# Half-width products in seven for the gate tiles of the first mixer and the up tiles of the second FFN, and a plain down projection behind them

## The chip, the cores and the metric

The kernel runs on one core of one Trainium2 chip. The metric is the device time of one execution in microseconds (us). Engines are named as in the profile: PE (TensorE, the matmuls), PEld (its weight loads), DVE (VectorE), ACT (ScalarE), POOL (GpSimd) and SP (SyncE, which here only issues the loads of weights).

## What is computed

The input is a row of 512 tokens with 1024 features, all in fp32. Two blocks follow each other. The change touches these lines of the first one:

```python
h = h + 0.5 * swiglu(rms_norm(h, ffn1_norm), ffn1_w1, ffn1_w3, ffn1_w2)
u = rms_norm(h, mix_norm)
s5_in, q, k, v, r, a_low, g_s5, g_gla = split(u @ w_in)      # g_s5, g_gla: 1024 columns each
...
merged = sigmoid(g_s5) * (y_s5 @ proj_s5) + sigmoid(g_gla) * (y_gla @ proj_gla)
h = h + merged @ w_out
h = h + 0.5 * swiglu(rms_norm(h, ffn2_norm), ffn2_w1, ffn2_w3, ffn2_w2)

def swiglu(x, w1, w3, w2):            # D_FF = 2816
    return (silu(x @ w1) * (x @ w3)) @ w2
```

The second block is another mixer and a third FFN; the change leaves them alone.

## The kernel before

Features lie on the partitions and tokens on the free axis, so that an activation of 1024 features is eight tiles of 128x512 and the 2816 features of an FFN are 22 such tiles. Every fp32 product is made of three fp32r matmuls (`mm3`): each operand is split into a rounded high part and the rest, and high by high, high by low and low by high are added up in PSUM. All of these matmuls have the line of one helper, L408. For weights the split costs work on two engines: SP loads a "raw" tile of up to 1024 columns (three buffers), ACT casts it to "wh" (four buffers), and DVE subtracts the cast from the raw tile and leaves "wl" (four buffers). The product of one output tile with eight input tiles is 24 matmuls of 512 columns into one of four PSUM banks (tag "mm").

The normalisation's factor rB is not applied to the inputs of a product (hgh, hgl: the input times the norm's weights, split) but when its result is read out of PSUM. So a tile of the second FFN (`up_tile`) is: 24 matmuls for w1, 24 for w3, DVE multiplies each by rB ("ua", "ub"), ACT makes silu of the first ("us"), DVE multiplies the two. A gate tile of the first mixer (`gate`) is 24 matmuls, a multiplication by rB on DVE and a sigmoid on ACT.

There is a second form of product in the kernel, `seven`: a block of two output tiles by two input tiles, with the 512 tokens cut in two halves, is a 2x2 matrix product of blocks, and it is made of seven half-width products (256 columns) in place of eight. Before the products, DVE makes sums and differences of the four weight blocks ("ws", two buffers) and of the two input tiles (T1 to T4; `Pairs.put`); after them, sums of the seven results. P7 and P4 share a PSUM bank, as do P5 and P3, and P1 and P2, so that the first of each must be read before the second starts. Before the change this form stands only in the down projections of the three FFNs: `gated` makes the up tiles in parts of four (`PARTS`), and each part of four tiles is multiplied by w2 in four `down_pair` of one `seven` each, spread between the next part's up tiles; the last six of the 22 tiles (`REST`) go plain.

The order of the instructions on each engine isn't that of the code. A recorder takes down every operation with a cost, and `schedule` is a list planner: it gives each engine the first operation by class (URGENT, MAIN, BACK) and program order whose inputs and buffers are ready by the costs. The order is static: on the chip each engine runs its list in order and waits for semaphores. In the first mixer the gate tiles are MAIN work, between which the small fp32 matmuls of the GLA branch (BACK) are laid one by one.

The stages lie in the trace as follows: first FFN to 312 us, first mixer to 695.5 (its gate tiles' matmuls from 490 to 598, then the S5 output, the two projections and w_out), second FFN to 1054, second mixer to 1417, third FFN to the end.

Of the kernel before, what the change touches and what calls it, by code (L numbers as in the profile page):

```python
# [1668 lines left out]
```

## Time and profile before

| | us |
|---|---|
| median of three runs | 1789.58 (1789.54 to 1789.81) |
| the profiled execution, its own time | 1789.26 |
| its span, first to last instruction | 1787.5 |
| PE busy | 1772.5 (99%) |
| DVE busy | 1344.0 (75%) |
| ACT busy | 889.4 (50%) |
| granted TensorE clock, mean | 0.997 |

A matmul's duration in the trace (395 ns for 512 columns) overlaps the next one's; what a matmul costs in a row of them is the distance between two starts. On DVE and ACT, too, an instruction often starts a little before the one ahead of it has ended. "Idle before, releaser" says how long an engine sat idle before a group of instructions and what ended that.

### The profile page before, as it was taken

Reading aid. Unit: us, or ns where it says so; the run is one execution under the profiler, and the core shown is the slowest. Engines: PE = TensorE matmul, PEld = TensorE weight load, DVE = VectorE, ACT = ScalarE, POOL = GpSimd, SP = SyncE. Lnnn points to the kernel's source line nnn. Section 1 sums busy time; section 2 is a strip of 40 time slices with the busy share of each in tenths; the row PEclk is TensorE's granted clock in tenths of the full one; section 3 lists DMA queues with packets and bytes.
Section 4 is the critical chain, followed back from the end, with each engine's and each line's share of the span. In section 5 each row is a group of like instructions: output and inputs, shape, how many; then the busy total and the mean of one; then the engine's idle time right before and its main releaser. Section 6 shows DMA issues by size and latency. Waiting matters only on the chain. (4 is left out here: it accounts for less than half of the span.)

```text
span 1787.5 us, 23941 instructions
## 1 busy us (share of the span) xinstructions
PE 1772.5 (99%) x9010; PEld 1510.7 (85%) x9010; DVE 1344.0 (75%) x2516; ACT 889.4 (50%) x1179; POOL 96.2 (5%) x180
## 2 busy tenths in 40 slices
PE   9999999999999999999999999999999999999997
PEld 7888888878888888888888888888888888888886
DVE  8899999659674475667777589788856578887875
ACT  6454444432853334333333354999953454554443
POOL 0011111211100000000000001000000000000000
PEclk9999999999999999999999999999999999999998
DMA  7455555665322342233333335232234444454551
GB/s 246 119 153 160 150 151 171 195 216 171 107 69 80 98 141 95 86 98 100 97 97 103 95 112 165 83 98 91 85 105 147 118 118 130 124 136 131 140 142 47
DMA packets 75636, 222.09 MB, mean 124 GB/s; under 512 B 8736, under 2 KB 17728, under 8 KB 75520
## 3 DMA queue, kind: packets, MB, share of 16 engines
q1 hardware_dynamic: 62304, 175.68, 30.4%
q0 software_dynamic: 13072, 44.87, 10.4%
q8 instruction: 71, 1.16, 0.3%
q14 instruction: 45, 0.37, 0.1%
q10 hardware_dynamic: 144, 0.00, 0.0%
HBM read 182.77 MB, written 15.73 MB: 111 GB/s over the span
## 5 line engine op out<-in xcount | busy, mean ns | idle before, releaser
L408 PE MATMUL mm<-hgh,wh 128*128 128x512 f32 x1528 | 602.9, 395 | 0.5 <-DVE ua L355 0.5
L408 PE MATMUL mm<-hgl,wh 128*128 128x512 f32 x1528 | 602.3, 394 | 0.0
L408 PE MATMUL mm<-hgh,wl 128*128 128x512 f32 x1520 | 598.9, 394 | 0.0
L400 ACT ACTIVATE wh<-raw 128x1024 fp32r<-128x1024 f32 (+2 forms) x315 | 310.0, 993 | 568.2 <-PE mm L408 322.5
L408 PEld LDWEIGHTS mm<-hgh,wh 128*128 128x128 f32 x1528 | 286.7, 188 | 58.4 <-DVE ua L355 0.9
L408 PEld LDWEIGHTS mm<-hgh,wl 128*128 128x128 f32 x1520 | 285.6, 188 | 58.5 <-issue 0.2
L408 PEld LDWEIGHTS mm<-hgl,wh 128*128 128x128 f32 x1528 | 286.5, 188 | 57.0 <-issue 0.2
L355 DVE TENSOR_TENSOR wl<-raw,wh 128x1024 fp32r<-128x1024 f32 (+2 forms) x272 | 306.6, 1128 | 34.0 <-ACT wh L400 33.4
L355 DVE TENSOR_TENSOR h<-mm,h 128x256 f32<-128x256 f32 (+1 forms) x134 | 66.2, 497 | 52.5 <-PE mm L408 51.6
L400 ACT ACTIVATE wh<-ws 128x1024 fp32r<-128x1024 f32 x48 | 50.7, 1056 | 83.1 <-PE mm L408 79.8
L400 ACT ACT_TABLE_LOAD x63 | 80.8, 1283 | 2.9 <-PEq L1659 1.2
L355 DVE TENSOR_TENSOR ub<-mm,rB 128x512 f32<-128x512 f32 x44 | 30.4, 691 | 64.0 <-PE mm L408 63.9
L355 DVE TENSOR_TENSOR ua<-mm,rB 128x512 f32<-128x512 f32 x54 | 37.3, 690 | 52.5 <-PE mm L408 51.0
L367 DVE SCALAR_TENSOR_TENSOR y<-t,vec,y 128x511 f32<-128x511 f32 x88 | 65.7, 747 | 7.8 <-ACT y L400 6.9
L421 POOL DMA_DIRECT2D wl<-raw x42 | 36.6, 872 | 605.4 <-ACT wl L400 464.1
L355 DVE TENSOR_TENSOR t<-mm,rB 128x512 f32<-128x512 f32 x44 | 30.4, 690 | 49.7 <-PE mm L408 49.5
L355 DVE TENSOR_TENSOR h<-h,mm 128x256 f32<-128x256 f32 x144 | 59.6, 414 | 1.6 <-PE mm L408 1.5
L355 DVE TENSOR_TENSOR wl<-ws,wh 128x1024 fp32r<-128x1024 f32 x48 | 58.6, 1221 | 1.8 <-ACT wh L400 1.8
L355 DVE TENSOR_TENSOR gate<-mm,rB 128x512 f32<-128x512 f32 x32 | 22.0, 688 | 44.1 <-PE mm L408 43.6
L408 PE MATMUL mm<-x1h,wl 128*128 128x256 f32 x192 | 54.3, 283 | 0.0
L408 PE MATMUL mm<-x1l,wh 128*128 128x256 f32 x192 | 54.3, 283 | 0.0
L408 PE MATMUL mm<-x1h,wh 128*128 128x256 f32 x192 | 54.3, 283 | 0.0
(358 smaller groups left out, 3404.6 us busy)
## 6 DMA issues: line engine op xcount, KB each, us to landing
raw<-in_ffn_w_dram SPq DMA_DIRECT2D x84, 512.0 KB, 3.5
raw<-in_w_in_dram SPq DMA_DIRECT2D x62, 512.0 KB, 3.4
raw<-in_w_up_dram SPq DMA_DIRECT2D x44, 512.0 KB, 3.8
wl<-raw POOLq DMA_DIRECT2D x42, 512.0 KB, 4.5
raw<-in_ffn_w_s_dram SPq DMA_DIRECT2D x32, 512.0 KB, 4.4
raw<-in_w_out_dram SPq DMA_DIRECT2D x16, 512.0 KB, 3.3
raw<-in_w_down_s_dram SPq DMA_DIRECT2D x16, 512.0 KB, 4.8
s5w<-dram POOLq DMA_DIRECT2D x28, 256.0 KB, 4.5
```

The lines of the kernel that those rows point to most:

```text
L355: R.op("dve", dve1(o), lambda: nc.vector.tensor_tensor(out=o, in0=a, in1=b, op=op), [o], [a, b])
L367: R.op("dve", dve1(o) + 0.06 * len(_aps(s)), lambda: nc.vector.scalar_tensor_tensor(out=o, in0=a, scalar=s, in1=b, op0=op0, op1=op1), [o], ...
L400: R.op("act", c, lambda: nc.scalar.activation(o, i, f, **kw), [o], _aps(i, scale, bias), table=TABLES.get(f), cls=cls, after=after)
L408: R.op("pe", c, lambda: nc.tensor.matmul(ps, a, b, start=start, stop=stop, **kw), [ps], [a, b])
L421: R.op("pool", 1.04, lambda: nc.gpsimd.dma_start(o, i, accum_op=ALU.add), [o], [i, o], nbytes=4.0 * _size(o) * o.shape[0], lat=2.5)
```

## The change

Two stages get the seven-product form where they had plain products, and one loses it.

- `forms` makes the sums of the eight normalised input tiles once for a stage: for each of the four pairs of tiles, DVE adds high and low part back together (fa, fb), makes T1 to T4 in four half-width operations, and ACT and DVE split them.
- `pair8` makes two output tiles with all eight inputs by seven products of 12 half-width matmuls each. It loads two raw tiles of 512 KB, makes two tiles of weight sums, and splits four weight tiles (HW1, HA, HW2, HB). P7, P4 and P1 are copied out of PSUM by ACT, the others are read by DVE.
- First mixer: gate tiles 0 to 3 stay plain, 4 to 15 are six `pair8`.
- Second FFN: of the 22 up tiles six stay plain; the other 16 are eight pairs, each a `pair8` for w1 and one for w3. Its down projection is plain throughout, in five parts (`DOWN`); a part's four pairs of output tiles are taken up one at a time after the following up tiles or `pair8`, the last part at the end.

The first and third FFN and the second mixer keep their code; the weights are laid out for the new loads.

```diff
+    def forms(xs, after):
+        res = []
+        cut = lambda hl, o: (hl[0][:, o:o + HALF], hl[1][:, o:o + HALF])
+        for a_, b_ in zip(xs[0::2], xs[1::2]):
+            a, b, t1, t2 = slot("fa"), slot("fb"), slot("t1"), slot("t2")
...
+            add(b, b_[0], b_[1])
+            sub(t1[:, 0:HALF], a[:, 0:HALF], a[:, HALF:])
+            sub(t1[:, HALF:], b[:, HALF:], a[:, HALF:])
+            stt(t2[:, 0:HALF], t1[:, 0:HALF], -1.0, b[:, HALF:], ALU.mult, ALU.subtract)
+            stt(t2[:, HALF:], t2[:, 0:HALF], -1.0, b[:, 0:HALF], ALU.mult, ALU.subtract)
+            h1, h2 = split(t1, "x1"), split(t2, "x2")
...
+    def pair8(src, xs, rB):
+        c = 512
+        r1, r2 = new("raw", "raw"), new("raw", "raw")
+        dma("sp", r1, src[:, 0:2 * c])
+        dma("sp", r2, src[:, 2 * c:4 * c])
+        w1 = new("ws", "ws")
...
+        tt(v2(w1), v2(r2), r1[:, 0:c].unsqueeze(1).to_broadcast([128, 2, c]), ALU.add)
+        HW1 = split_of(w1, 2 * c)
+        HA = split_of(r2, 2 * c)
+        w2 = new("ws", "ws")
+        add(w2[:, 0:c], w1[:, 0:c], r2[:, c:2 * c])
+        add(w2[:, c:2 * c], w2[:, 0:c], r1[:, c:2 * c])
+        HW2 = split_of(w2, 2 * c)
+        HB = split_of(r1[:, c:2 * c], c)
...
+        def p6(ps):
+            add(V, ps, V)
+            tt(x3, x3, v3, ALU.add)
+            stt(x1, x1, -1.0, rB, ALU.mult, ALU.mult)
+        def p3(ps):
+            add(x0[:, hi], ps, V)
+            mul(x0[:, hi], x0[:, hi], rB[:, hi])
+        read = {"P7": lambda ps: act(x1[:, hi], ps, AF.Copy), "P5": lambda ps: add(x1[:, hi], ps, x1[:, hi]),
+                "P4": lambda ps: act(x1[:, lo], ps, AF.Copy), "P1": lambda ps: act(V, ps, AF.Copy),
+                "P6": p6, "P3": p3, "P2": lambda ps: mul(x0[:, lo], ps, rB[:, lo])}
+        for key, (h, l), o, x, bank, more in (
+                ("P7", HW1, c, "T3", "D", False), ("P5", HW1, 0, "T1", "C", False),
+                ("P4", HA, 0, "T4", "D", True), ("P1", HA, c, "B11", "A", False),
+                ("P6", HW2, 0, "T2", "B", False), ("P3", HW2, c, "B22", "C", True),
+                ("P2", HB, 0, "B21", "A", True)):
...
+    UP0 = 6
+    DOWN = ((0, 4), (4, 8), (8, 12), (12, 16), (16, NFF))
+    def swiglu_pairs(hg, rB, h, done):
...
+        xs = forms(hg, [rB])
+        for n in range(UP0):
+            a.append(split(up_tile("ffn2_w1", "ffn2_w3", n, hg, rB), "g"))
...
+        for i in range((NFF - UP0) // 2):
+            us = pair8(A["ffn2_w1_g"][i], xs, rB)
+            for u in us:
+                act(u, u, AF.Silu)
+            if jobs:
+                down(*jobs.pop(0))
+            vs = pair8(A["ffn2_w3_g"][i], xs, rB)
...
-    swiglu("ffn2_w1", "ffn2_w3", "ffn2_w2", hg0, rB, h, both)
+    swiglu_pairs(hg0, rB, h, both)
...
-    g5 = [gate(i) for i in range(8)]
-    gg = [gate(8 + i) for i in range(8)]
+    xs = e.forms(hg, [G["r"][3]])
+    for i in range(6):
+        for x in e.pair8(e.A["w_in_g"][i], xs, rB):
+            act(x, x, AF.Sigmoid)
+            gates.append(x)
```

How the lists of the engines look at the places of which the prediction speaks (in brackets the engines and DMA queues whose semaphores a row waits for). First DVE while the later gate tiles are made; x are a gate pair's two tiles, V the shared partial sum, ws the weight sums. Before:

```order
L355 TENSOR_TENSOR ygl_1064<-o_1057,ygh_1063 128x512 [waits DMASW5_49,Activation_49]
L355 TENSOR_TENSOR gate_1105<-mm_1106,rB_813 128x512 [waits PE_49]
L355 TENSOR_TENSOR wl_1129<-raw_1127,wh_1128 128x1024 [waits DMAHW5_49,Activation_49]
L355 TENSOR_TENSOR gate_1110<-mm_1111,rB_813 128x512 [waits PE_49]
L355 TENSOR_TENSOR wl_1134<-raw_1132,wh_1133 128x1024 [waits DMAHW6_49,Activation_49]
L355 TENSOR_TENSOR gate_1115<-mm_1116,rB_813 128x512 [waits PE_49]
L355 TENSOR_TENSOR wl_1139<-raw_1137,wh_1138 128x1024 [waits DMAHW7_49,Activation_49]
```

Now:

```order
L355 TENSOR_TENSOR wl_1178<-ws_1176,wh_1177 128x1024 [waits PE_49,Activation_49]
L355 TENSOR_TENSOR V_1169<-mm_1173,V_1169 128x256 [waits PE_49,Activation_49]
L355 TENSOR_TENSOR ws_1181<-ws_1181,raw_1174 128x512 [waits DVE_49]
L355 TENSOR_TENSOR x_1071_1168<-x_1071_1168,V_1169 128x512 [waits DVE_49]
L355 TENSOR_TENSOR x_1070_1167<-mm_1171,V_1169 128x256 [waits PE_49]
L367 SCALAR_TENSOR_TENSOR x_1071_1168<-x_1071_1168,rB_813 128x512 [waits DVE_49]
L355 TENSOR_TENSOR x_1070_1167<-x_1070_1167,rB_813 128x256 [waits DVE_49]
L355 TENSOR_TENSOR wl_1183<-ws_1181,wh_1182 128x1024 [waits Activation_49]
L355 TENSOR_TENSOR x_1070_1167<-mm_1172,rB_813 128x256 [waits PE_49]
L355 TENSOR_TENSOR wl_1185<-raw_1174,wh_1184 128x512
L355 TENSOR_TENSOR x_1090_1187<-mm_1190,x_1090_1187 128x256 [waits PE_49,Activation_49]
```

Where a gate tile was one read of PSUM and one subtraction, two gate tiles are now fourteen operations.

Next DVE and PE while the first gate pair's products run; rs and aux_1034 are a GLA norm factor and its broadcast by PE, S the GLA state. DVE now:

```order
L355 TENSOR_TENSOR x_1033_1130<-mm_1133,x_1033_1130 128x256 [waits PE_49,Activation_49]
L355 TENSOR_TENSOR rs_1033<-rs_1033 128x4 [waits DVE_49]
L367 SCALAR_TENSOR_TENSOR S_1038<-S_1038,tiny_938,aux_1042 64x128
L355 TENSOR_TENSOR wl_1140<-ws_1138,wh_1139 128x1024 [waits Activation_49]
L355 TENSOR_TENSOR ygl_1028<-o_1021,ygh_1027 128x512 [waits Activation_49]
L367 SCALAR_TENSOR_TENSOR rs_1033<-rs_1033,ms_1032 128x4 [waits DVE_49]
L367 SCALAR_TENSOR_TENSOR S_1038<-S_1038,tiny_938,aux_1042 64x128
L367 SCALAR_TENSOR_TENSOR rs_1033<-rs_1033 128x4 [waits DVE_49]
L388 COPY_PREDICATED sc_1045<-smask,aux_1043 128x128 [waits Pool_49]
L355 TENSOR_TENSOR rs_1033<-rs_1033 128x4 [waits DVE_49]
L388 COPY_PREDICATED sc_1046<-smask,aux_1043 128x128 [waits Pool_49]
L367 SCALAR_TENSOR_TENSOR rs_1033<-rs_1033,ms_1032 128x4 [waits DVE_49]
```

PE now, in P6 of that pair:

```order
L408 MATMUL mm_1135<-x2h_1107,wl_1126 128x256
L411 MATMUL aux_1034<-cst,rs_1033 128x128 [waits DVE_49]
L408 MATMUL mm_1135<-x2h_1115,wh_1125 128x256
L411 MATMUL aux_1034<-cst,rs_1033 128x128
L408 MATMUL mm_1135<-x2l_1116,wh_1125 128x256
```

Before, this broadcast stood among the plain gate tiles, and rs_1033 behind short operations alone; now the subtraction wl_1140 of the next pair stands in the middle of its chain.

ACT in the later gate pairs; the copies from mm_1170 are P7 and P4, V is P1:

```order
L400 ACTIVATE wh_1165<-raw_1155 128x512 [waits DMAHW1_49,PE_49,Activation_49]
L400 ACTIVATE x_1052_1149<-x_1052_1149 128x512 [waits DVE_49,Activation_49]
L400 ACTIVATE x_1071_1168<-mm_1170 128x256 [waits PE_49]
L400 ACTIVATE x_1051_1148<-x_1051_1148 128x512 [waits DVE_49]
L400 ACTIVATE wh_1179<-raw_1175 128x1024 [waits DMAHW4_49,PE_49,Activation_49]
L400 ACTIVATE x_1071_1168<-mm_1170 128x256 [waits PE_49]
L400 ACTIVATE wh_1177<-ws_1176 128x1024 [waits DVE_49,PE_49]
L400 ACTIVATE V_1169<-mm_1172 128x256 [waits PE_49]
L400 ACTIVATE wh_1184<-raw_1174 128x512 [waits DMAHW3_49,PE_49,Activation_49]
L400 ACTIVATE wh_1182<-ws_1181 128x1024 [waits DVE_49,PE_49,Activation_49]
```

Before, with gate tiles alone:

```order
L400 ACTIVATE wh_1108<-raw_1107 128x1024 [waits DMAHW1_49,PE_49]
L400 ACTIVATE ygh_1027<-o_1021 128x512 [waits DVE_49]
L400 ACTIVATE gate_1085<-gate_1085 128x512 [waits DVE_49]
L400 ACTIVATE ygh_1035<-o_1029 128x512 [waits DVE_49]
L400 ACTIVATE wh_1113<-raw_1112 128x1024 [waits DMAHW2_49,PE_49]
```

A pair's sigmoids (x_1052, x_1051), which need the last DVE operations of the pair ahead, now stand in front of and behind the copy of P7 that frees a bank for P4.

Last, the start of the second FFN on DVE; ua and ub are the first reads of its up products, t and x1l, x2l are T1, T2 and their low parts. Before:

```order
L355 TENSOR_TENSOR wl_1336<-raw_1334,wh_1335 128x1024 [waits DMAHW7_49,PE_49,Activation_49]
L355 TENSOR_TENSOR ua_1309<-mm_1301,rB_1298 128x512 [waits Activation_49]
L355 TENSOR_TENSOR ub_1311<-mm_1305,rB_1298 128x512 [waits PE_49]
L367 SCALAR_TENSOR_TENSOR ub_1311<-ub_1311,us_1310 128x512 [waits DVE_49,Activation_49]
L355 TENSOR_TENSOR wl_1340<-raw_1338,wh_1339 128x1024 [waits DMAHW0_49,Activation_49]
```

Now, at the same place (the rows of `forms` begin behind wl_1448 and go on for 28 rows):

```order
L355 TENSOR_TENSOR x1l_1408<-t_1307_1405,x1h_1407 128x512 [waits Activation_49]
L367 SCALAR_TENSOR_TENSOR t_1316_1414<-t_1316_1414,fb_1412 128x256 [waits DVE_49]
L355 TENSOR_TENSOR x2l_1410<-t_1308_1406,x2h_1409 128x512 [waits Activation_49]
L355 TENSOR_TENSOR x1l_1416<-t_1315_1413,x1h_1415 128x512
L355 TENSOR_TENSOR x2l_1418<-t_1316_1414,x2h_1417 128x512 [waits Activation_49]
L355 TENSOR_TENSOR ua_1427<-mm_1419,rB_1384 128x512
L355 TENSOR_TENSOR ub_1429<-mm_1423,rB_1384 128x512 [waits PE_49]
```

Of the 32 DVE operations of `forms`, all but the four additions for fb stand in one row between wl_1448 and the first read of a PSUM bank: 12 of 512 columns and 16 of 256.

## Rows read from the trace of the kernel before

**Rows 1.** The page: busy time, share of the span and instructions of each engine.

```profile
PE 1772.5 (99%) x9010; PEld 1510.7 (85%) x9010; DVE 1344.0 (75%) x2516; ACT 889.4 (50%) x1179; POOL 96.2 (5%) x180
```

**Rows 2.** Groups on PE: busy, mean ns, idle time before them and its releaser.

```profile
L408 PE MATMUL mm<-hgh,wh 128*128 128x512 f32 x1520 | 599.8, 395 | 0.5 <-DVE ua L355 0.5
...
L411 PE MATMUL aux<-cst,rs 128*128 128x128 f32 x40 | 8.4, 280 | 2.5 <-DVE rs L367 2.5
```

**Rows 3.** Windows: busy time (and instructions) of each engine, granted clock, DMA share.

```profile
505.00:560.00 55.00, 54.94 (x300) 46.24 (x300) 36.59 (x112) 20.90 (x34) 0.53 (x1) 1.00 0.20 65
560.00:598.00 38.00, 38.00 (x169) 31.49 (x168) 13.36 (x14) 10.94 (x15) 0.00 (x0) 1.00 0.31 97
...
700.00:1050.00 350.00, 350.00 (x1865) 303.46 (x1866) 249.99 (x421) 129.97 (x170) 0.00 (x0) 1.00 0.31 98
```

**Rows 4.** Timeline of PE, plain up tiles: start, duration, line, operation.

```profile
727.09 0.39 PE L408 MATMUL mm<-hgh,wh 128*128 128x512 f32 x1
...
732.52 0.39 PE L408 MATMUL mm<-hgh,wh 128*128 128x512 f32 x1
```

**Rows 5.** Timeline of PE, half-width products of the down projection.

```profile
800.10 0.28 PE L408 MATMUL mm<-x1h,wh 128*128 128x256 f32 x1
...
801.54 0.28 PE L408 MATMUL mm<-x2h,wh 128*128 128x256 f32 x1
```

**Rows 6.** Groups on DVE by shape: busy, mean ns, idle before.

```profile
L355 DVE TENSOR_TENSOR wl<-ws,wh 128x1024 fp32r<-128x1024 f32 x48 | 58.6, 1221 | 1.8 <-ACT wh L400 1.8
...
L355 DVE TENSOR_TENSOR x1l<-t,x1h 128x512 fp32r<-128x512 f32 x24 | 16.4, 682 | 0.0
```

**Rows 7.** Timeline of DVE among half-width products: start, duration.

```profile
800.99 1.22 DVE L355 TENSOR_TENSOR wl<-raw,wh 128x1024 fp32r<-128x1024 f32 x1
802.12 0.42 DVE L355 TENSOR_TENSOR h<-h,mm 128x256 f32<-128x256 f32 x1
...
803.20 0.42 DVE L355 TENSOR_TENSOR t<-ub,ub 128x256 f32<-128x256 f32 x1
803.53 0.68 DVE L355 TENSOR_TENSOR xbl<-ub,xbh 128x512 fp32r<-128x512 f32 x1
804.14 0.41 DVE L355 TENSOR_TENSOR h<-h,mm 128x256 f32<-128x256 f32 x1
```

**Rows 8.** Timeline of ACT in the same stretch: a cast, a PSUM copy.

```profile
800.37 0.37 ACT L400 ACTIVATE V<-mm 128x256 f32<-128x256 f32 x1
...
804.98 1.05 ACT L400 ACTIVATE wh<-ws 128x1024 fp32r<-128x1024 f32 x1
```

**Rows 9.** Timeline of PE in the gate tiles: fp32 insertions, each with an ordinary matmul.

```profile
514.48 0.38 PE L408 MATMUL aux<-sc,v 128*128 128x128 f32 x2
...
514.93 0.38 PE L408 MATMUL aux<-sc,v 128*128 128x128 f32 x2
```

**Rows 10.** Timeline of DVE in the gate tiles: norm factor and state.

```profile
523.47 0.16 DVE L367 SCALAR_TENSOR_TENSOR rs<-rs 128x4 f32<-128x4 f32 x1
523.66 0.16 DVE L355 TENSOR_TENSOR rs<-rs 128x4 f32<-128x4 f32 x1
```

**Rows 11.** Timeline of PE at the start of the second FFN.

```profile
695.75 0.39 PE L408 MATMUL mm<-hgh,wh 128*128 128x512 f32 x1
...
699.83 0.95 PE L408 MATMUL aux<-cst,ssum 128*128 128x2 f32 x8
...
703.73 0.60 PE L411 MATMUL aux<-cst,rs 128*128 128x128 f32 x4
```

**Rows 12.** Timeline of DVE at the same place: last split ahead, first read.

```profile
703.23 1.23 DVE L355 TENSOR_TENSOR wl<-raw,wh 128x1024 fp32r<-128x1024 f32 x1
704.99 0.69 DVE L355 TENSOR_TENSOR ua<-mm,rB 128x512 f32<-128x512 f32 x1 [0.54 <-ACT rB L400]
```

**Rows 13.** DMA issues: count, KB, us from issue to landing.

```profile
raw<-in_w_in_dram SPq DMA_DIRECT2D x62, 512.0 KB, 3.4
...
raw<-in_ffn_w_s_dram SPq DMA_DIRECT2D x32, 512.0 KB, 4.4
```

More of the change, by code (lines that the diff above doesn't have):

```diff
@@ L565, in put, with split_of @@
                 T2=cut(h2, 0), T4=cut(h2, HALF)))
-    def split_of(src, c):
+    def split_of(src, c, moved=False):
         h = new("wh", "wh", F32R)
@@ L570, in split_of @@
         act(h[:, :c], src, AF.Copy)
-        sub(l[:, :c], src, h[:, :c])
-        return h, l
+        if moved:
+            act(l[:, :c], h[:, :c], AF.Copy, scale=-1.0)
+            dma_add(l[:, :c], src)
+        else:
+            sub(l[:, :c], src, h[:, :c])
+        return h, l
+    def forms(xs, after):
[3 more added lines that the diff above has]
+            a, b, t1, t2 = slot("fa"), slot("fb"), slot("t1"), slot("t2")
+            R.op("dve", dve1(a), lambda a=a, a_=a_: nc.vector.tensor_tensor(out=a, in0=a_[0], in1=a_[1], op=ALU.add),
+                 [a], [a_[0], a_[1]], after=after)
+            add(b, b_[0], b_[1])
[4 more added lines that the diff above has]
+            h1, h2 = split(t1, "x1"), split(t2, "x2")
+            res.append(dict(B11=cut(a_, 0), B21=cut(b_, 0), B22=cut(b_, HALF), T1=cut(h1, 0), T3=cut(h1, HALF),
+                            T2=cut(h2, 0), T4=cut(h2, HALF)))
+        return res
@@ new lines, in pair8 @@
+    def pair8(src, xs, rB):
[4 more added lines that the diff above has]
+        w1 = new("ws", "ws")
+        v2 = lambda t: t.rearrange("p (a b) -> p a b", a=2)
+        tt(v2(w1), v2(r2), r1[:, 0:c].unsqueeze(1).to_broadcast([128, 2, c]), ALU.add)
[6 more added lines that the diff above has]
+        HB = split_of(r1[:, c:2 * c], c)
+        x0, x1, V = slot("x0"), slot("x1"), new("sv", "V")
+        lo, hi = slice(0, HALF), slice(HALF, S)
+        x3 = v2(x1)
+        v3 = V.unsqueeze(1).to_broadcast([128, 2, HALF])
+        def p6(ps):
[8 more added lines that the diff above has]
+                "P6": p6, "P3": p3, "P2": lambda ps: mul(x0[:, lo], ps, rB[:, lo])}
+        ps = {}
+        for key, (h, l), o, x, bank, more in (
[3 more added lines that the diff above has]
+                ("P2", HB, 0, "B21", "A", True)):
+            if not more:
+                ps[bank] = mmps()
+            p = ps[bank][:, 0:HALF]
+            for k, part in enumerate(xs):
+                cc = slice(o + k * 128, o + k * 128 + 128)
+                mm3(p, (h[:, cc], l[:, cc]), part[x], k == 0 and not more, k == len(xs) - 1, more)
+            with cls(URGENT):
+                read[key](p)
+        return x0, x1
@@ L764, in gated, with down, queue @@
         return rest
+    UP0 = 6
+    DOWN = ((0, 4), (4, 8), (8, 12), (12, 16), (16, NFF))
+    def swiglu_pairs(hg, rB, h, done):
+        a, jobs = [], []
+        def down(p, n):
+            k0, k1 = DOWN[p]
+            for i, ps in enumerate(linear_pair("ffn2_w2_%d" % p, n, a[k0:k1])):
+                add(h[n + i], ps, h[n + i])
+        def queue():
+            p = [k1 for _, k1 in DOWN].index(len(a)) if len(a) in [k1 for _, k1 in DOWN[:-1]] else None
+            if p is not None:
+                jobs.extend((p, n) for n in range(0, KD, 2))
+        xs = forms(hg, [rB])
+        for n in range(UP0):
+            a.append(split(up_tile("ffn2_w1", "ffn2_w3", n, hg, rB), "g"))
+            queue()
+            if jobs:
[4 more added lines that the diff above has]
+                act(u, u, AF.Silu)
+            if jobs:
+                down(*jobs.pop(0))
+            vs = pair8(A["ffn2_w3_g"][i], xs, rB)
+            for u, v in zip(us, vs):
+                stt(v, v, 0.5, u, ALU.mult, ALU.mult)
+                a.append(split(v, "g"))
+            if jobs:
+                down(*jobs.pop(0))
+            queue()
+        while jobs:
+            down(*jobs.pop(0))
+        p = len(DOWN) - 1
+        for n in range(KD):
+            ps = linear("ffn2_w2_%d" % p, n, a[DOWN[p][0]:])
+            with cls(URGENT):
+                add(h[n], ps, h[n])
+                done(h[n], n)
     def swiglu(w1, w3, w2, hg, rB, h, done, up0=()):
@@ L1157, in mixer1 @@
         gla_run(e, G, yg)
-    def gate(i):
+    gates = []
+    for i in range(4):
         x = slot("gate")
@@ L1162, in gate @@
         act(x, x, AF.Sigmoid)
-        return x
-    g5 = [gate(i) for i in range(8)]
-    gg = [gate(8 + i) for i in range(8)]
-    y5 = []
-    zs = [e.split(z, "zs") for z in zs5]
+        gates.append(x)
[3 more added lines that the diff above has]
+            act(x, x, AF.Sigmoid)
+            gates.append(x)
+    g5, gg = gates[:8], gates[8:]
+    y5 = []
+    zs = []
+    for z in zs5:
+        zh, zl = slot("zsh", F32R), slot("zsl", F32R)
+        act(zh, z, AF.Copy, after=[gg[3]])
+        sub(zl, z, zh)
+        zs.append((zh, zl))
     for n in (0, 2):
@@ L1597, in arrays_of @@
     s5, q, k, v, rr, al, g5, gg = (w[:, cut[i]:cut[i + 1]] for i in range(8))
-    r["w_in"] = _wlay(np.concatenate([s5, q, k, rr, g5, gg], 1))
+    r["w_in"] = _wlay(np.concatenate([s5, q, k, rr, g5[:, :512]], 1))
+    r["w_in_g"] = _wpairs(np.concatenate([g5[:, 512:], gg], 1), ((0, 8),))
     r["w_v"] = np.ascontiguousarray(v.reshape(8, 128, 512).transpose(1, 0, 2).reshape(128, 4096))
```

9 lines of the change are left out of this document (7 added, 2 removed).

## The prediction

> **What bounds the kernel now.** I read the page's busy times first. PE is busy 1772.5 us of a span of 1787.5 [rows 1], and the idle time listed ahead of its groups is small: half a microsecond ahead of the plain products, 2.5 ahead of the 40 broadcasts of norm factors [rows 2]. So PE's work is the time, and what to read next is whether that holds in the two stages that change. It does: PE is busy 54.94 of 55 us and 38.00 of 38 among the gate tiles and all of 350 us in the second FFN, at a granted clock of 1.00, the 2.4 GHz level [rows 3]. DVE is the nearest other engine: 36.59 of 55 and 13.36 of 38 in the two windows of the gates, 249.99 of 350 in the FFN [rows 3]. A PE instruction saved is therefore worth its pace until DVE, which gets work in both stages, is late.
>
> **What a matmul costs.** Its duration in the trace overlaps the next one, so I take starts. From 727.09 to 732.52 there are 24 matmuls of 512 columns: 5.43 us, 0.2265 each [rows 4]. From 800.10 to 801.54 there are 12 of 256: 1.44, 0.120 each [rows 5]. Half the columns cost 0.53 of the time. A block of two by two tiles is then 12 x 0.2265 = 2.72 plain and 21 x 0.120 = 2.52 in seven: 0.20 saved, 7%, not the eighth that the count of products says.
>
> **PE, the whole change.** Of 512 columns: 16 up tiles go with 48 each (768), 12 gates with 24 (288), and the plain down projection brings 16 x 8 x 3 = 384: 672 fewer, -152.2 us. Of 256 columns: 16 pair8 of 84 in the FFN (1344) and six in the mixer (504) come, and the FFN's 16 down_pair of 42 (672) go: 1176 more, +141.1. The sum is -11.1 us, some -4.7 of it in the gates and -6.4 in the FFN. All of it lies on the engine that sets the end.
>
> The Trainium skill ("TensorE: Matmul & The Clock Gate", section "Back-to-back issue gap") gives isolated gaps of 518 and 262 cycles for 512 and 256 columns. At 2.4 GHz that is an estimate of 216 and 109 ns, and by it the sum would be -16.7 us. The trace disagrees: 226.5 and 120 ns, so about 11 ns per matmul more at either width, and the sum goes by the trace.
>
> **DVE, where the cover has to hold.** Durations of one are 1.22 us for 1024 columns and 0.68 for 512 [rows 6], 0.42 for 256 [rows 7]; but in a row of independent operations the next starts earlier, after 1.13, 0.61 and 0.33 [rows 7]. I take these steps as the lower bound and the durations as the upper one; the steps are from a stretch of the same mix of operations, so I stay near them.
>
> In the FFN an iteration (two pair8, two down pairs) is on DVE 10 operations of 1024, 18 of 512 and 10 of 256: 25.6 us by steps, 28.7 by durations. PE takes 168 x 0.120 + 48 x 0.2265 = 31.0. Covered at either bound, so I add nothing.
>
> Among the gates it is tight. From the start of forms to the first read of the sixth pair DVE has 23 of 1024, 52 of 512, 42 of 256 and 39 short ones of some 0.2 [rows 10]: 26.0 + 31.7 + 13.9 + 7.8 = 79.4 by steps, 28.1 + 35.4 + 17.6 + 7.8 = 88.9 by durations. PE in that stretch has 96 x 0.2265 + 444 x 0.120 = 75.0 and about 38 fp32 insertions of the GLA branch; one with its ordinary matmul takes 0.45 [rows 9], so 0.22 alone: 83.4. DVE would use 95% or 107% of it. The worst place is early: PE's broadcast of rs_1033 stands in P6 of the first pair, after four plain tiles, 57 half-width matmuls and 18 insertions: 21.7 + 6.8 + 4.0 = 32.5 us from the first gate tile. DVE reaches the end of the rs_1033 chain after the last r tile's read (0.8), then 6 of 1024, 22 of 512, 17 of 256 and 34 short ones: 6.8 + 13.4 + 5.6 and 5 to 8, by how far two chains of short ones interleave; that is 31.6 to 34.6, and up to 38 by durations. Behind the waiting broadcast all of PE is queued. I take +1.2, with 0 to 5.5 as ends.
>
> **ACT.** P4 overwrites the bank that ACT's copy of P7 frees. PE covers that with P5, 12 x 0.120 = 1.44 us. The copy needs the tail of P7's last matmul (0.28 - 0.12 [rows 5]) and 0.37 [rows 8], 0.53; with a cast of 1.05 [rows 8] just begun it is 1.6. So 0 to 0.2 us for each of 22, 0 to 4; I take 0, since casts mostly wait for buffers that PE frees elsewhere.
>
> **The ends of the FFN.** At its start four plain products fill the four banks: 695.75 + 96 x 0.2265 + 0.8 and 0.35 for the norm's own matmuls [rows 11] = 718.6, when PE needs ua's bank. The split at 703.23 ends its step at 704.36, and before the change ua came next, at 704.99 [rows 12]. Now 28 operations of forms come first: 12 x 0.61 + 16 x 0.33 = 12.6 and ua's 0.69, 717.7; by durations 720.0; with ACT's casts of T1 and T2 queued behind weight casts that wait for PE, later still. I take +0.3 (0 to 3). At its end the last w1 pair has no down pair behind it: two pair8 in a row, 168 x 0.120 = 20.2 us of PE, against twice four operations of 1024, five of 512 and five of 256 on DVE, 18.4 by steps and 20.8 by durations: +0.3 (0 to 2).
>
> **Sum.** 1789.26 for the profiled execution, - 11.1 + 1.2 + 0.3 + 0.3 = 1780.0; the median of the runs is 0.3 above that execution, so 1780.3. Without any stall 1778.5.
>
> **Rivals.** First, VectorE becomes the bound: its operations go by durations. For it: dependent pairs and semaphore waits do lengthen steps, and most PSUM reads in a pair8 depend on the one ahead. Against it: [rows 7] has the same reads, casts' rests and sums in a row, and they overlap. It would cost 88.9 + 0.8 - 83.4 = 6.3 in the gates and 1.4 + 2 at the FFN's ends, in place of 1.8: 1788.2 at full weight, 1782.5 to 1786 for a part.
>
> The Trainium skill ("VectorE: DVE Perf Modes", "The DRAIN you can't avoid") says that the next operation does not start until the pipe is empty, though it grants that one not held starts earlier. Read strictly it is this rival. By that sentence the trace disagrees: at 802.12 an operation starts 0.09 us before the one of 800.99 ends [rows 7].
>
> Second, the saving doesn't come, because raw tiles come late. A pair8 takes two of three raw buffers, and in the FFN only 2.4 to 4.4 us of DVE work stand between the last use of a buffer and the sum that needs its next load; a load lands in 3.4 us, in 4.4 with rows cut out of a longer one [rows 13]. DVE then waits up to 2 us per pair8, 4 of its 5.4 spare us in an iteration. With two loads at once landing in 6 us it would be 7.2, 1.8 too many, 12.6 over seven iterations: 1791, or 1787 for half of that. Against it: what is late there is needed only a down pair (5.4 us) later, and the DMA engines are busy 0.31 [rows 3].
>
> Third, slower: ACT's list is in order, and ahead of P7's copy stand sigmoid, silu or split of the pair before, which wait for DVE's last operations on that pair. If DVE is late, the copy is, and PE waits at P4 in every pair8. It decides from 11.1 / 22 = 0.5 us per pair8; at 1 us per pair8 it is 1789.6 - 11.1 + 22 = 1800. For it: cover is only 1.44 us, and DVE has 5% spare in the gates. Against it: in the FFN, 16 of the 22, DVE has 18% spare.
>
> **How the numbers follow.** The forecast (1777.5 to 1782.5) gets 0.62, VectorE in part (1782.5 to 1786) 0.17, late loads or VectorE in full (1786 to 1793) 0.11, slower (above 1793) 0.10. What a measurement can tell from no change is about 0.2%, 3.6 us: 1786 to 1793. So faster 0.79, same 0.11, slower 0.10. From 1777.5 to 1788 lie 0.82.
>
> **What would show it.** Right: PE busy falls by about 11 us, the pace stays 0.2265 and 0.120, PE's idle time grows by 1 to 3 us, most of it ahead of broadcasts of rs in the gates. VectorE as bound: idle PE ahead of half-width groups, released by DVE, and DVE above 95% in the gates. Slower: idle ahead of mm<-x2h, released by ACT. Late loads: DVE idle ahead of ws, released by DMA, and PE idle behind it. A half-width pace above 0.125 in pair8 would refute the first step.

## The result, and the profile after

The changed kernel takes 1780.25 us (median of four runs, 1779.6 to 1780.48), the kernel before 1789.61 beside it: a ratio of 0.9945 with a 95% interval of 0.9933 to 0.9957. The profiled execution took 1779.6, with a span of 1777.8 and a mean granted clock of 0.997.

The page's busy line of the changed kernel, to be read against [rows 1]:

```profile
PE 1760.8 (99%) x9514; PEld 1525.4 (86%) x9514; DVE 1422.5 (80%) x2604; ACT 929.0 (52%) x1263; POOL 96.1 (5%) x180
```

PE has 504 instructions more and 11.7 us less; DVE has 78.5 us more. The windows that answer to [rows 3] (busy time and instructions of PE, PEld, DVE, ACT, POOL, then granted clock and DMA share), shortened at the ends because the stages now end earlier:

```profile
505.00:560.00 55.00, 55.00 (x378) 51.19 (x377) 53.39 (x115) 30.35 (x46) 1.05 (x2) 1.00 0.22 72
560.00:594.00 34.00, 34.00 (x291) 34.00 (x290) 31.23 (x68) 20.66 (x36) 0.00 (x0) 1.00 0.34 98
700.00:1040.00 340.00, 340.00 (x2135) 308.99 (x2134) 276.19 (x401) 156.73 (x222) 0.00 (x0) 1.00 0.31 100
```

PE is never idle in either changed stage, although DVE is at 97% and 92% in the gate windows. Where the time went is read from the first matmul of each stage. Before, the S5 output and the second mixer (the second FFN, at 695.75, is in [rows 11]):

```profile
597.83 0.39 PE L408 MATMUL mm<-zsh,wh 128*128 128x512 f32 x1
...
1050.12 0.39 PE L408 MATMUL mm<-hgh,wh 128*128 128x512 f32 x1
```

In the changed kernel the S5 output, the second FFN and the second mixer:

```profile
594.22 0.40 PE L408 MATMUL mm<-zsh,wh 128*128 128x512 f32 x1
...
692.66 0.39 PE L408 MATMUL mm<-hgh,wh 128*128 128x512 f32 x1
...
1040.62 0.39 PE L408 MATMUL mm<-hgh,wh 128*128 128x512 f32 x1
```

So the second FFN takes 348.0 us in place of 354.4 and gives 6.4. (Its end before the change is 1050.12 and not the 1054 of the section on the kernel before.) The mixer up to there gives 3.1 (the first matmul of w_out, too, moves from 652.23 to 649.14). One wait ahead of the gates is new and costs 1.66, so that 4.75 is left for the gates, by subtraction. The waits of PE in the changed kernel (total, times, longest):

```profile
PE aux L411 <- DVE rs L367: 2.5, 1, 2.5
PE aux L408 <- ACT ke L400: 1.5, 1, 1.5
PE mm L408 <- ACT ph L400: 1.1, 1, 1.1
...
PE mm L408 <- DVE ua L355: 0.5, 1, 0.5
```

The first and the last stand in the kernel before as well, with the same sizes [rows 2]. The wait for ph (0.4 before) is in the first 8 us of the program and moves nothing: PE passes the wait for ua at 30.22, before at 30.23. The wait for ke is new. Its place on PE (start, duration, operation, idle before and releaser):

```profile
471.88 0.39 PE L408 MATMUL mm<-hgl,wh 128*128 128x512 f32 x1
473.77 0.70 PE L408 MATMUL aux<-v,ke 128*128 128x256 f32 x2 [1.50 <-ACT ke L400]
```

and the list of ACT ahead of it:

```profile
469.23 0.72 ACT L400 ACTIVATE zw<-zw,cst 128x512 f32<-128x512 f32 x1
469.97 1.28 ACT L400 ACT_TABLE_LOAD   x1
471.26 1.13 ACT L400 ACTIVATE zs<-yf 128x512 f32<-128x512 f32 x1
472.18 1.06 ACT L400 ACTIVATE wh<-raw 128x1024 fp32r<-128x1024 f32 x1
473.14 1.20 ACT L400 ACTIVATE ke<-aux 64x512 f32<-64x512 f32 x2
```

Two starts are 1.89 us apart where plain matmuls stand 0.2265 apart: 1.66 lost. The copy of ke (k of the GLA branch, transposed) starts at 473.14 behind a table load, a GELU of 1.13 and a cast. In the kernel before, the same ke matmul stands at 491.13 and has no wait.

### The profile page after: what moved, and what is told of

The parts are those of the page before. It is cut to its first block, busy times and chain, and to the rows that moved or that the text cites. A ratio compares the mean times of both kernels' runs of the same rounds, so it can differ in the third digit from the quotient of the medians.

```text
span 1777.8 us, 25154 instructions
## 1 busy us (share of the span) xinstructions
PE 1760.8 (99%) x9514; PEld 1525.4 (86%) x9514; DVE 1422.5 (80%) x2604; ACT 929.0 (52%) x1263; POOL 96.1 (5%) x180
## 5 line engine op out<-in xcount | busy, mean ns | idle before, releaser
L408 PE MATMUL mm<-hgh,wh 128*128 128x512 f32 (+1 forms) x1440 | 539.2, 374 | 0.5 <-DVE ua L355 0.5
L408 PE MATMUL mm<-hgl,wh 128*128 128x512 f32 (+1 forms) x1440 | 539.1, 374 | 0.0
L400 ACT ACTIVATE wh<-raw 128x1024 fp32r<-128x1024 f32 (+3 forms) x315 | 304.1, 974 | 446.6 <-PE mm L408 314.2
L408 PE MATMUL mm<-hgh,wl 128*128 128x512 f32 (+1 forms) x1432 | 535.9, 374 | 0.0
L355 DVE TENSOR_TENSOR wl<-raw,wh 128x1024 fp32r<-128x1024 f32 (+3 forms) x272 | 298.9, 1100 | 43.4 <-ACT wh L400 42.5
L408 PE MATMUL mm<-gl,wh 128*128 128x512 f32 x260 | 101.3, 390 | 0.0
L408 PE MATMUL mm<-gh,wl 128*128 128x512 f32 x260 | 101.2, 389 | 0.0
L408 PE MATMUL mm<-gh,wh 128*128 128x512 f32 x260 | 100.7, 390 | 0.0
L408 PE MATMUL mm<-x2l,wh 128*128 128x256 f32 x304 | 85.6, 285 | 0.0
L408 PE MATMUL mm<-x2h,wl 128*128 128x256 f32 x304 | 84.2, 285 | 0.0
```

What stands on the lines that cost most here:

```text
L355: R.op("dve", dve1(o), lambda: nc.vector.tensor_tensor(out=o, in0=a, in1=b, op=op), [o], [a, b])
L400: R.op("act", c, lambda: nc.scalar.activation(o, i, f, **kw), [o], _aps(i, scale, bias), table=TABLES.get(f), cls=cls, after=after)
L408: R.op("pe", c, lambda: nc.tensor.matmul(ps, a, b, start=start, stop=stop, **kw), [ps], [a, b])
```

## The experiments

### Which part brings what

**Gates alone.** The changed kernel with the old second FFN:

```diff
-    swiglu_pairs(hg0, rB, h, both)
+    swiglu("ffn2_w1", "ffn2_w3", "ffn2_w2", hg0, rB, h, both)
```

> The gate tiles by pairs, the second FFN as before. Theory A (each stage gives what its matmuls save, and what is missing is one wait of 1.5 us for ACT's ke, ahead of the gate tiles): PE saves 288 x 0.2265 - 504 x 0.120 = 4.7, the ke wait takes 1.5 back, 1786.4 us against 1789.6, idle of about 1.5 ahead of aux<-v,ke and none in the gates. Rival B (VectorE is late in the gates): 1788 or more, idle PE ahead of half-width groups released by DVE. Rival C (the gates give nothing, the FFN all of it): 1789.6.

Measured: 1787.13 against 1789.87 of the kernel before, ratio 0.9987 (0.9978 to 0.9997). The wait for ke is there with 1.5 us, and PE waits for nothing among the gate tiles. The time is 0.7 above theory A's figure. In the profiled execution PE passes the wait for ua 1.1 us later than before (31.30), which the edit doesn't touch; from there to w_out it is 3.1 us faster, as in the whole change.

**Second FFN alone.** The changed kernel with the old gate tiles and the old split of zs:

```diff
-    xs = e.forms(hg, [G["r"][3]])
-    for i in range(6):
-        for x in e.pair8(e.A["w_in_g"][i], xs, rB):
...
+    g5 = [gate(i) for i in range(8)]
+    gg = [gate(8 + i) for i in range(8)]
...
+    zs = [e.split(z, "zs") for z in zs5]
```

> The second FFN by pairs, the gate tiles as before. Theory A: 384 x 0.2265 - 672 x 0.120 = 6.3 saved and no new wait, 1783.2 us, no idle of 1.5 ahead of aux<-v,ke. If stalls at the FFN's start and end exist as I had priced them (0.3 each), 1783.8. Rival C: 1780.3, all of the gain here.

Measured: 1783.42, ratio 0.9967 (0.9954 to 0.998), and no wait for ke. The gains of the two, 2.7 and 6.5 us, add up to 9.2; the whole change gives 9.4.

**The hold on zs alone.** The change also holds back the splits of the GELU's results (zs) until the gate tile gg[3] is read. Here that line is put into the kernel before, and nothing else:

```diff
-    zs = [e.split(z, "zs") for z in zs5]
+    for z in zs5:
...
+        act(zh, z, AF.Copy, after=[gg[3]])
```

> The kernel before with one edit: the split of the S5 outputs zs is held back until the gate tile gg[3], as the change does. No product is made otherwise. Theory A (holding zs back lets the list put the GLA branch's ke earlier, behind an ACT that isn't done): 1.5 us of idle ahead of aux<-v,ke, 1791.1 us. Rival D (the wait comes from the load that forms and pair8 put on DVE and ACT): no such wait, 1789.6.

Measured: 1792.09, ratio 1.0011 (1.0002 to 1.0021), with the wait for ke at 1.5 us. So neither pairs nor VectorE's load are needed for the wait. The time is 1.0 above theory A's; in the profiled execution PE passes the wait for ua 2.3 us later than before (32.53), and from there to w_out the hold costs 1.85. With the splits out of the way the planner puts the GLA steps earlier (the matmul on ke at 475.97 in place of 491.13), and on the chip ke is late. Why the plan is early by just that much wasn't measured; it counts 0.52 us for the GELU ahead of ke, which takes 1.13.

**ke planned later.** In the changed kernel the planner is told that the copy of ke takes 1.6 us longer; the computation and every instruction stay the same, only the order moves:

```diff
-            act(x[cr], pt[cr], AF.Copy)
+            act(x[cr], pt[cr], AF.Copy, extra=1.6)
```

> The changed kernel, with the cost of ACT's two ke copies in the list's planning raised by 1.6, so that PE's matmuls on ke stand 7 places (1.6 us) later; the work is the same. Theory A: the wait ahead of aux<-v,ke falls from 1.5 to under 0.3 and the time to 1778.8 to 1779.1. Rival E (PE's idle time only moves to the next GLA step, since that branch's chain is what is late): idle elsewhere in 465 to 530, time 1780.2 as it was.

Measured: 1778.36 (1777.4 to 1779.49), ratio 0.9937 (0.9922 to 0.9952). The wait for ke is gone. The first matmul of the S5 output stands at 592.64 in place of 594.22, that of w_out at 647.07 in place of 649.14. Of these 2.1 us 1.66 are the wait for ke and 0.2 a wait for S that is gone with it; the rest wasn't traced. The kernel is faster than the one before and the changed one. With four runs from 1777.4 to 1779.49 its median is good to about 1 us.

### How much VectorE has to spare

The prediction counted VectorE's spare time by its share of PE's. The next runs add operations that write the same values again, without telling the planner, so that the order of all lists is that of the changed kernel.

**Twice in the gates.** The subtraction that makes the low part of HA is done twice in each of the six gate pairs:

```diff
-            sub(l[:, :c], src, h[:, :c])
+            R.op("dve", dve1(l[:, :c]), lambda: [nc.vector.tensor_tensor(
+                out=l[:, :c], in0=src, in1=h[:, :c], op=ALU.subtract) for _ in range(times)], [l[:, :c]], [src, h[:, :c]])
...
-        HA = split_of(r2, 2 * c)
+        HA = split_of(r2, 2 * c, times=times)
...
-        for x in e.pair8(e.A["w_in_g"][i], xs, rB):
+        for x in e.pair8(e.A["w_in_g"][i], xs, rB, times=2):
```

> The changed kernel; in the six pair8 of the gate tiles DVE makes the subtraction of HA twice (one more operation of 1024 columns, 1.13 us by steps, in the same place of the list). Theory A (DVE goes by steps and is at 95% there): it becomes 1.02 to 1.03 of PE's time, so some 2 to 4 us longer, 1782.5 to 1784, with idle PE ahead of half-width groups that DVE releases. Rival F (DVE has slack that the tally doesn't see): under 0.5 us. Rival B (it was the bound already): all of 6 x 1.13 = 6.8, 1787.

Measured: 1787.89, ratio 0.9986 (0.9975 to 0.9997): 7.6 us for six operations of 1.13, where theory A expected 2 to 4 and rival B 6.8. Its windows in the gates, and a stretch behind the last wait:

```profile
540.00:560.00 20.00, 19.15 (x160) 18.94 (x159) 19.93 (x30) 11.15 (x19) 0.00 (x0) 1.00 0.32 106
560.00:580.00 20.00, 19.43 (x161) 19.11 (x160) 19.93 (x32) 11.70 (x18) 0.00 (x0) 1.00 0.33 106
580.00:604.00 24.00, 22.81 (x165) 22.48 (x165) 19.53 (x50) 11.96 (x22) 0.00 (x0) 0.86 0.31 89
```

```profile
593.30:599.90 6.60, 6.60 (x32) 6.60 (x32) 4.07 (x25) 1.72 (x3) 0.00 (x0) 0.50 0.33 98
```

DVE has hardly a gap from 540 to 580, and PE waits for it, or for ACT behind it, five times between 523 and 592, 3.2 us in total. VectorE is the bound here, as in the prediction's first rival. From 593.3 to 599.9 PE's clock is at half as well. Matmul by matmul against the changed kernel the mixer is 7.9 us longer in the profiled execution, and 3.1 of that come in this slow stretch. The other 4.8 are what 6.8 us of work on DVE cost directly, so about 2 of the 4 us that the prediction's sum left over (83.4 - 79.4) could be had. Without the clock theory A's 2 to 4 us would have been 1 us short.

**Twice in the second FFN.** The same in the 16 pairs there (the w1 pairs and the w3 pairs), where DVE is busy 163.80 of 190 us from 800 to 990 in the changed kernel. In place of the gates' line:

```diff
-            us = pair8(A["ffn2_w1_g"][i], xs, rB)
+            us = pair8(A["ffn2_w1_g"][i], xs, rB, times=2)
...
-            vs = pair8(A["ffn2_w3_g"][i], xs, rB)
+            vs = pair8(A["ffn2_w3_g"][i], xs, rB, times=2)
```

> The changed kernel; in the 16 pair8 of the second FFN DVE makes the subtraction of HA twice. Theory A: DVE's 25.6 us of an iteration become 27.9 of PE's 31.0, so nothing but the two ends, 1780.2 to 1781. Rival B (bound by DVE already): 16 x 1.13 = 18 longer.

Measured: 1788.33, ratio 0.9989 (0.9978 to 1.0001): 8.1 us where at most 1 was expected. The waits of PE and of DVE for these (of DVE in the FFN alone), and the window:

```profile
PE mm L408 <- DVE wl L575: 4.5, 4, 2.8
```

```profile
DVE ws L355 <- DMA raw<-in_ffn_w_g_dram: 9.8, 8, 2.2
```

```profile
800.00:990.00 190.00, 188.20 (x1308) 176.01 (x1307) 171.45 (x243) 84.81 (x121) 0.00 (x0) 1.00 0.30 102
```

PE waits for DVE while DVE has 10% idle. What it idles for is the landing of raw tiles: 9.8 us in eight waits, where the changed kernel has one of 0.7. One of them, from the sums that free a buffer over SP's two loads to the sum that waits:

```profile
912.93 1.41 DVE L355 TENSOR_TENSOR ws<-ws,raw 128x512 f32<-128x512 f32 x2
...
913.68 1.02 SPq L416 DMA_DIRECT2D raw<-in_ffn_w_g_dram  x2
...
919.96 1.23 DVE L355 TENSOR_TENSOR ws<-raw,raw 128x1024 f32<-128x1024 f32 x1 [2.18 <-DMA raw<-in_ffn_w_g_dram]
```

The second load is issued at 914.37, when the sum has freed its buffer, and lands 5.6 us later. In the changed kernel the same load is issued at 910.00 and lands 4.9 later, at 914.89, and the sum that needs it starts at 915.34 without a wait. A busier DVE frees a raw buffer later, its next load is issued later, and DVE then waits for its own delay. Spare time that is spent on such waits can't be given to other work.

**Four times in the second FFN.** The same lines with another number:

```diff
-            us = pair8(A["ffn2_w1_g"][i], xs, rB)
+            us = pair8(A["ffn2_w1_g"][i], xs, rB, times=4)
...
-            vs = pair8(A["ffn2_w3_g"][i], xs, rB)
+            vs = pair8(A["ffn2_w3_g"][i], xs, rB, times=4)
```

> The changed kernel; in the 16 pair8 of the second FFN DVE makes the subtraction of HA four times: 25.6 + 6.8 = 32.4 us in an iteration against 31.0 of PE. Theory A: 1.4 longer in each of eight, 1790 to 1793, above the kernel before. If an operation had to wait for the end of the one ahead (28.7 + 7.3 = 36.0): 5 longer in each, 1820.

Measured: 1828.15 (two runs), ratio 1.0215 (1.0185 to 1.0245), 48 us, above both figures that were expected. The first repetition's 18.1 us of work cost 8.1, the 36 of the second and third cost 40, some of it by a lower clock (0.991 in the mean). PE waits 27.2 us for wl in 15 places. DVE, busy 172.69 us of the 190 from 800 to 990, waits 11.6 us for raw tiles in the stage: its list with these waits in it sets the pace.

**The other weights.** HA's repetition keeps a raw tile in use for 1.13 us longer. To see whether that is the cause, HW1's subtraction, which reads the sums and no raw tile, is done twice instead:

```diff
-        HW1 = split_of(w1, 2 * c)
+        HW1 = split_of(w1, 2 * c, times=times)
```

> The changed kernel; in the 16 pair8 of the second FFN DVE makes the subtraction of HW1 twice, not that of HA: the same 16 x 1.13 us of DVE work, but on an operation that reads weight sums and no raw tile. Theory G (what costs in the run with HA made twice is that a raw tile is held longer, so the next load lands late and DVE sits idle for it): DVE's waits for raw loads stay under 4 us (9.8 there) and the time at 1781 to 1784. Theory H (the amount of DVE work costs, wherever it stands): 1786 to 1789 as there, with the same waits.

Measured: 1788.19, ratio 0.9988 (0.9977 to 0.9998), 4.1 us of waits for wl in five places and 15.1 us of waits of DVE for raw tiles. The price is the same at both places of the list, and theory G (under 4 us of waits for raw tiles, 1781 to 1784) falls: holding HA's raw tile isn't the cause. That DVE's list as a whole comes late, and the raw tiles with it, fits both runs. A fourth raw buffer would tell whether the late loads or the order of the list alone keep DVE from catching up; this wasn't tried and stays open.

**Half an operation.** If there is a margin that is spent first, less than the margin should cost nothing. In the changed kernel two such margins can be read. One pair in the second FFN (the whole core by start):

```profile
912.98 0.28 PE L408 MATMUL mm<-x2h,wh 128*128 128x256 f32 x1
...
913.11 1.06 ACT L400 ACTIVATE wh<-ws 128x1024 fp32r<-128x1024 f32 x1 [0.99 <-PE mm L408]
...
914.20 1.22 DVE L355 TENSOR_TENSOR wl<-ws,wh 128x1024 fp32r<-128x1024 f32 x1 [0.53 <-ACT wh L400]
...
915.86 0.28 PE L408 MATMUL mm<-x2h,wh 128*128 128x256 f32 x1
...
916.10 0.28 PE L408 MATMUL mm<-x2h,wl 128*128 128x256 f32 x1
```

At 912.98 PE begins P4, which frees the buffer for ACT's cast of HW2; DVE's subtraction follows the cast and ends at 915.42. PE has made P4 and P1 by 915.86 (24 x 0.120) and needs the low part at 916.10: 0.68 us later. That margin, 0.67 to 0.68, is the same in eight of the 16 pairs. The smallest in the FFN, 0.52, stands at 993.64, at the last w1 pair. The edit repeats only half of HA's subtraction, 0.61 us:

```diff
+                out=l[:, :w], in0=src[:, :w], in1=h[:, :w], op=ALU.subtract) for w in ((c, c // 2)[:times])], [l[:, :c]], [src, h[:, :c]])
```

> The 16 pair8 of the second FFN with half of the HA subtraction (512 of 1024 columns) done a second time, writing the same values: 16 further DVE operations of 0.61 us, at the same places of the same list as the full repetition, which was 16 of 1.13 and cost 8.1 us over the changed kernel's 1780.25. Theory M (a margin): PE gives VectorE 0.67 us per pair8 before HW2's low part is late, and only what exceeds it costs. Then the full repetition's price is 16 x (1.13 - 0.67) = 7.4 and some for the clock after a wait, as measured, and 0.61 is below the margin in nearly all pairs: 1780.2 to 1781.7, and no wait of PE for VectorE's wl above 0.5 us. Theory P (in proportion): VectorE's list waits for its operands in a fixed pattern, each added microsecond costs the same share, 8.1 / 18.1 = 0.45. Then 9.8 us more on VectorE cost 4.4: 1784 to 1785.5.

Measured: 1782.6 (1781.21 to 1784.05), ratio 0.996 (0.9946 to 0.9973), between the two theories' figures. The trace tells more. PE has one new wait in the whole run:

```profile
PE mm L408 <- DVE wl L575: 1.5, 1, 1.5
```

and it stands at that last w1 pair, whose w3 pair follows with no down projection between them. On PE, then DVE's list ahead of it:

```profile
995.27 0.28 PE L408 MATMUL mm<-hgh,wh 128*128 128x256 f32 x1
997.01 0.39 PE L408 MATMUL mm<-x2h,wl 128*128 128x256 f32 x1 [1.46 <-DVE wl L575]
```

```profile
980.19 1.23 DVE L355 TENSOR_TENSOR ws<-raw,raw 128x1024 f32<-128x1024 f32 x1 [1.38 <-DMA raw<-in_ffn_w_g_dram]
...
995.73 1.22 DVE L575 TENSOR_TENSOR wl<-ws,wh 128x1024 fp32r<-128x1024 f32 x1
```

In the changed kernel the first of these two rows has 0.75 idle ahead of it in place of 1.38. From there to 996.95 DVE doesn't rest, and two further half operations lie in between: 0.63 + 2 x 0.61 against a margin of 0.52. At this pair 1.7 us are lost of the 2.2 by which the second FFN is longer than in the changed kernel; the other 0.5 goes in slower steps at three places (818, 870 and 933) without a listed wait. So a price in proportion, 4.4 spread over the pairs, falls. Theory M's figure falls too. In six of the eight pairs the margin is 0.67 as before. In the pair shown above DVE's subtraction now stands here, and PE needs its result at 916.97:

```profile
915.08 1.23 DVE L575 TENSOR_TENSOR wl<-ws,wh 128x1024 fp32r<-128x1024 f32 x1 [0.53 <-ACT wh L400]
```

There the cast waits for PE and the subtraction for the cast, in both kernels, so the 0.67 is what PE's own pace leaves and the half operation doesn't reach it. In the other two pairs 0.06 is left of it. So a margin is spent first, but it isn't a fresh 0.67 for each pair. Delays pass on from pair to pair (the wait for the raw tile at 980.19 grew from 0.75 to 1.38), and a stretch without a down projection is where they come out; in the full repetition, too, PE's longest wait stands there (2.83 us, at 1001.08) and only three others are seen.

### How much the copy of P7 has to spare

The prediction gave ACT's copy of P7 a cover of 1.44 us against 0.53, so 0.9 to spare. Here ACT makes the copy four times in all 22 pairs:

```diff
+        def p7(ps):
+            o = x1[:, hi]
+            R.op("act", 0.09 + 256 / 1200.0 - 0.04, lambda: [nc.scalar.activation(o, ps, AF.Copy) for _ in range(4)],
+                 [o], [ps], table=TABLES.get(AF.Copy))
```

> The changed kernel; in all 22 pair8 ACT copies P7 out of its bank four times, so that P4 may start 3 x 0.37 us later. Theory A (PE covers the copy with P5's 1.44 us, and the copy alone takes 0.53): 0.53 + 1.1 to 1.3 is 0.2 to 0.4 too much, 22 x that = 4 to 9 us longer, 1784.5 to 1789, with idle PE ahead of mm<-x2h that ACT releases. If P4 weren't bound to that copy: 1780.2.

Measured: 1793.23, ratio 1.0021 (1.001 to 1.0032): 13.0 us, above the 4 to 9 of theory A. Waits, then one pair on ACT and PE:

```profile
PE mm L408 <- ACT x L628: 6.6, 22, 0.5
```

```profile
920.70 1.64 ACT L628 ACTIVATE x<-mm 128x256 f32<-128x256 f32 x4 [0.60 <-PE mm L408]
```

```profile
921.82 0.28 PE L408 MATMUL mm<-x1h,wl 128*128 128x256 f32 x1
922.39 0.39 PE L408 MATMUL mm<-x2h,wh 128*128 128x256 f32 x1 [0.29 <-ACT x L628]
922.61 0.28 PE L408 MATMUL mm<-x2l,wh 128*128 128x256 f32 x1
```

Four copies take 1.64 us, three more thus 1.25. PE starts P4 0.57 behind the matmul ahead of it and not 0.12, and the next one 0.22 and not 0.12: 0.55 lost, 22 times, 12.1 of the 13.0. The delay at P4 itself is 0.45, so 1.25 - 0.45 = 0.8 was free. The mechanism of the third rival is thus real and priced, and the change stands 0.8 us away from it in every pair.

### How far the form can be taken

Both runs have ke planned later. The first makes 18 of the 22 up tiles by pairs and leaves four plain, the second makes 20 and leaves two:

```diff
-    UP0 = 6
+    UP0 = 4
```

> The changed kernel with the later ke matmuls and with 18 of 22 up tiles of the second FFN by pairs (four plain ones ahead in place of six). Theory A: two more pair8 save 2 x (48 x 0.2265 - 84 x 0.120) = 1.6 on PE: 1778.4 - 1.6 = 1776.8. Theory H: without the down pairs that lie between them DVE isn't covered (9.2 to 10.4 us a pair8 against PE's 10.1), 1778 to 1780.

Measured: 1776.24 (1775.99 to 1776.49), ratio 0.9924 (0.9908 to 0.9941), and PE's waits are those of the run with six plain tiles, but for 0.7 us more at the start of the program. The second FFN is 1.53 us shorter than with six plain tiles, of 1.6 expected, and theory H falls. It is the fastest of all kernels here.

```diff
-    UP0 = 6
+    UP0 = 2
```

> The same with two plain up tiles and 20 by pairs. Theory A: four more pair8, -3.2: 1775.2. Against it: forms' 12.6 us of DVE and four banks are at the stage's start, two plain tiles give DVE 21.8 us for that and the first pair's weights, and the first pair8s come without down pairs; a wait of 2 to 4 us there and a half-clock stretch behind it would make it 1777 to 1780.

Measured: 1783.66 (1781.98 to 1785.69), ratio 0.9965 (0.9952 to 0.9978), above both figures that were expected (1775.2, and 1777 to 1780). In the profiled execution (1781.98) PE waits eight times between 716 and 774, 4.4 us in total, and nowhere else in the FFN; the first of them, among others:

```profile
716.92 0.39 PE L408 MATMUL mm<-x1h,wh 128*128 128x256 f32 x1 [0.76 <-DVE ub L355]
...
720.78 0.39 PE L408 MATMUL mm<-x2h,wl 128*128 128x256 f32 x1 [0.63 <-DVE wl L355]
...
728.27 0.38 PE L408 MATMUL mm<-x1h,wh 128*128 128x256 f32 x1 [0.74 <-ACT wh L400]
```

Two plain up tiles (96 x 0.2265 = 21.7 us of PE) are not enough to hide the 28 operations of `forms` and the first pair's weights; four are, without a wait in the FFN.

## Why the prediction was right, point by point

**The pace of a matmul, and PE's sum.** Right to about half a microsecond. Predicted were -4.7 in the gates and -6.4 in the FFN. The FFN measures -6.4. The gates' -4.75 is what the wait for ke leaves; where that wait is gone (ke planned later) the time from the wait for ua (30.23 before, 30.43 there) to w_out falls from 622.0 to 616.6, 5.4, of which 0.3 is the wait for S. The pace in a pair is the one read from the down projection [rows 5]: 24 matmuls from 912.98 to 915.86, 0.120 each. By the isolated gaps that the Trainium skill states ("TensorE: Matmul & The Clock Gate", section "Back-to-back issue gap") the estimate was -16.7, so here the measured pace decided.

**DVE's share.** Right. Predicted 95% of PE in the gates by steps; from 527 to 594 DVE is busy 63.29 of 67 us, 94.5%. In the FFN 25.6 of 31.0, 83%, was predicted by steps and 93% by durations; from 800 to 990 it is 86%. The steps of [rows 7] were the better bound. The sign named for VectorE as the bound, DVE above 95% in the gates, came as well (97% from 505 to 560), with PE never idle; the share alone doesn't tell the two apart.

**The broadcast of rs_1033, +1.2 (0 to 5.5).** Mis-sized: 0. Both sides arrive together. DVE's last step of the chain, and the broadcast on PE:

```profile
534.22 0.16 DVE L367 SCALAR_TENSOR_TENSOR rs<-rs 128x4 f32<-128x4 f32 x1
```

```profile
534.43 0.32 PE L411 MATMUL aux<-cst,rs 128*128 128x128 f32 x1
```

The chain ends at 534.38 and PE takes the broadcast 0.05 later, 0.21 behind the matmul ahead of it. The lower end of the range was the right one; 1.2 was taken as a middle, without a row.

**The ends of the FFN, +0.3 each (0 to 3, 0 to 2).** Both 0. PE waits at neither (the listed wait for ua is the first FFN's, at 30.22). At the start it was close: DVE's first read ends at 715.57, and PE begins to overwrite that bank at 715.84, 0.27 later, where the forecast's sum by steps left 0.9 (718.6 - 717.7). DVE first, then PE:

```profile
714.89 0.68 DVE L355 TENSOR_TENSOR ua<-mm,rB 128x512 f32<-128x512 f32 x1
```

```profile
715.84 0.40 PE L408 MATMUL mm<-hgh,wh 128*128 128x512 f32 x1
```

At the end the place was seen rightly: two pairs without a down projection between them have the smallest margin of the stage, 0.52 us, and the half operation came out exactly there.

**ACT's copy of P7, 0.** Right; its 1.44 and 0.53 leave 0.9 to spare, measured 0.8.

**What the prediction lacked.** The hold on zs, a line of the change that stands neither in the diff shown ahead of it nor in its sum, takes 1.66 us at a place 27 us ahead of the first gate tile. So PE's idle time did grow by 2.0 us (15.0 to 17.0), within the 1 to 3 that were named, but not ahead of broadcasts of rs in the gates. That the 1.66 lies near the 1.8 of stalls that didn't come is chance: the median of 1780.25 beside 1780.3 has two errors that cancel. Without either the kernel takes 1778.36, beside "without any stall 1778.5".

**The rivals.** VectorE by durations, late raw tiles and the late copy of P7 did not happen. All three are near. Six more operations of 1.13 in the gates make the first, sixteen in the FFN the second, and 0.8 us per pair the third. The prediction's "18% spare" of DVE in the FFN was the wrong measure of how near: by it, one more operation in each pair would have been free, and that expectation missed by 7 us.

## What to carry to other kernels

Price a rearranged product by the distance of starts in a row of such matmuls, not by counting products, and cost every line of a diff that changes an order, also where it adds no work. The spare time of an engine beside the bound is not its idle share. Look for the place where its result and the bound's need stand closest, read that margin in microseconds, and ask whether the loads that it releases move along with it. A stretch in which the covering plain work is missing (the first and the last step of such a stage) is where the margin runs out first.
